# Shift and scale of the first stage as TensorE products with two conditioning columns, in a diffusion block on one core

## The chip, the cores and the metric

The kernel runs on one core of one Trainium2 chip. The metric is the time of one execution on the device in microseconds, as the median of several executions. The execution that the profiler took is a separate one; its own time stands beside them below.

## The reference, cut to what matters

One layer of a diffusion backbone: 1024 latent tokens `x` and 256 context tokens `ctx`, width 1024. Ahead of everything stands an adaptive shift and scale: the conditioning vectors `c` (latent) and `c_ctx` (context) go through SiLU and a matrix `w_ada` of 1024 by 6144, which gives six vectors of 1024; the first two are the shift and the scale of the token mixer's input.

```python
silu_c = jax.nn.silu(c)
silu_cc = jax.nn.silu(c_ctx)
sh_m, sc_m, g_m, sh_f, sc_f, g_f = jnp.split((silu_c @ w_ada[l] + b_ada[l])[:, None, :], 6, axis=-1)
csh_m, csc_m, ... = jnp.split(silu_cc @ w_ada[l] + b_ada[l], 6, axis=-1)
y, y_c = token_mixer(x * (1.0 + sc_m) + sh_m, xc * (1.0 + csc_m) + csh_m, w_in[l], ...)
```

The mixer begins with one large input projection of the modulated tokens, `h @ w_in` (59 blocks of 128 output channels), whose parts feed neighbourhood attention, a recurrent branch and a gated branch; a merge, a norm and a gated feed-forward follow. The latent stream needs all six vectors, the context only the first two, since it is dropped after the mixer.

## The kernel before, in words

Activations lie with 128 channels on the partitions and tokens along the free axis, so the 1024 channels are eight tiles, numbered k = 0 to 7. Every number that enters a large product is split into a high part and a low part (`hh` and `hl` for the latent tile, `ch` and `cl` for the context tile, `wh` and `wl` for a weight block), and each product is three matmuls: high by high, low by high, high by low.

`phase0a` is the first stage. For each tile k it loads two blocks `w` of 128 rows of the transposed `w_ada` (the scale's and the shift's), and the tiles `x` and `xc`. The four numbers per channel (`mod`: scale and shift, each for latent and context) come from VectorE: `ada_row` multiplies a block of 128 by 1024 with a copy of SiLU(c) or SiLU(c_ctx) on all partitions (`cb`) and sums along the row. ScalarE then writes `hh` (rounded) and overwrites `x` with the modulated value, and GpSimd takes the difference, `hl`. The loop also begins the first projections as the tiles come: `FIRST` holds blocks 36 to 39, one of which is loaded and split in each of the passes k = 0 to 3 (`L234`, `L237`), and their products are accumulated in PSUM at lines L306 to L308. Three of these pairs of accumulators come from the six banks called `d`, the fourth from the two called `gr`.

After the loop the other projections run in the order of the list `ms`, each with lines L220 to L222; ScalarE evicts them (L444, L526 and others), VectorE shifts and mixes them along the tokens, and side work for the recurrent branch is put into TensorE's stream behind a later projection. VectorE also works off the other 32 blocks of `w_ada` there, two tiles `wa` in flight, with the same `ada_row`.

A scheduler decides in which order each engine gets its instructions when the program is built. Each engine takes its own in that order and waits where a semaphore says so. Loads are issued by the SyncE queue, in order as well. Tiles come from pools with a fixed number of buffers: 6 for `w5` (the `w` blocks here), 2 for `x`, 2 for `xc`, 2 for `wr` (raw weights), 2 banks for `gr`.

Of the kernel before, what the change touches and what calls it, by code (L numbers as in the profile page):

```python
# [15 lines left out]
P = 128  # L16
D = 1024
S = 1024
CT = 256
NT = S + CT  # L20
KT = D // P
# [7 lines left out]
COLS = (24, 32, 32, 24)  # L29
BOFF = {(0, 0): 0, (0, 1): 264, (0, 3): 616, (1, 0): 880, (1, 1): 1168, (1, 3): 1552}  # L30
NBIAS = 1840
FIRST = (36, 37, 38, 39)
LATE = 3
NWA, NW5, NT2 = 2, 6, 8
LEAD, LAG, AHEAD = 2, 2, 5
NPP, NPT = 4, 3
SIDE = 16
# [19 lines left out]
class Kern:  # L57
# [178 lines left out]
            hi_eng.tensor_copy(hi, src)  # L236
        (lo_eng or nc.vector).tensor_tensor(lo, src, hi.bitcast(F32), ALU.subtract)  # L237

    def ada_row(self, w, q, start, o, out):
        self.nc.vector.tensor_tensor_reduce(out, w, self.cb[q], 1.0, start, ALU.mult, ALU.add, o)  # L240


    def phase0a(self):
        nc, a, c, v = self.nc, self.a, self.c, self.v
        tp, hp = self.tp, self.hp
        self.cb = []
        one = self.bp.tile([1, P], F32, name="one")
        nc.vector.memset(one, 1.0)
        for q in range(2):
            t = (self.bp if q else tp).tile([P, D], F32, name=f"cb{q}")  # L250
            if q == 0:
                nc.sync.dma_start(t, a["crow"][:, 0:D].to_broadcast([P, D]))
                nc.scalar.activation(t, t, AF.Silu)
            for i in range(0, D * q, 512):
                cr = self.t2()
                nc.sync.dma_start(cr[0:1], a["crow"][:, D * q + i:D * q + i + 512])
                ps = self.dps()
                nc.tensor.matmul(ps, one, cr[0:1], start=True, stop=True)
                nc.scalar.activation(t[:, i:i + 512], ps, AF.Silu)
            self.cb.append(t)  # L260
        self.h = []
        self.hc = []
        bada = v("bada")
        first = {}
        for k in range(KT):
            x = self.bp.tile([P, S], F32, name="x", tag="x", bufs=2)
            xc = self.bp.tile([P, CT], F32, name="xc", tag="xc", bufs=2)
            m = self.cp.tile([P, 4], F32, name=f"mod{k}")
            w = [self.w5()[:, 0:D] for _ in range(2)]
            for i in range(2):  # L270
                nc.sync.dma_start(w[i], a["wada"][8 - 8 * i + k])
            for q in range(2):
                for i, b in enumerate((c["bsc"], bada)):
                    junk = w[i] if q else self.bp.tile([P, D], F32, name="junk", tag="junk", bufs=1)
                    self.ada_row(w[i], q, b[:, k:k + 1], m[:, 2 * i + q:2 * i + q + 1], junk)
            nc.sync.dma_start(x, a["xT"][k])
            nc.sync.dma_start(xc, a["cT"][k])
            hh = hp.tile([P, S], F32R, name=f"hh{k}")
            hl = hp.tile([P, S], F32R, name=f"hl{k}")
            ch = tp.tile([P, CT], F32R, name=f"ch{k}")  # L280
            cl = tp.tile([P, CT], F32R, name=f"cl{k}")
            for (xi, hi, lo, q, n) in ((x, hh, hl, 0, S), (xc, ch, cl, 1, CT)):
                sc_, sh_ = m[:, q:q + 1], m[:, 2 + q:3 + q]
                nc.scalar.activation(hi, xi, AF.Identity, scale=sc_, bias=sh_)
                nc.scalar.activation(xi, xi, AF.Identity, scale=sc_, bias=sh_)
                nc.gpsimd.tensor_tensor(lo, xi, hi.bitcast(F32), ALU.subtract)
            self.h.append((hh, hl))
            self.hc.append((ch, cl))
            if k < 4:
                z = FIRST[k]  # L290
                raw = self.raw()
                nc.sync.dma_start(raw, a["win"][z])
                w = [self.bp.tile([P, D], F32R, name=f"w{k}{i}") if k >= 2 else
                     self.wp.tile([P, D], F32R, name=n, tag=n, bufs=2) for i, n in enumerate(("wh", "wl"))]
                self.split(w[0], w[1], raw, nc.gpsimd)
                pss = [self.dps() for _ in range(2)] if k < 3 else [
                    self.ps.tile([P, 512], F32, name="gr", tag="gr", bufs=self.ngr) for _ in range(2)]
                first[z] = w + [pss]
            for i, (z, (wh, wl, pss)) in enumerate(first.items()):
                for k2 in range(0 if i == k else k, k + 1):  # L300
                    q = slice(P * k2, P * k2 + P)
                    hh, hl = self.h[k2]
                    xs = (self.hc[k2], (hh[:, 0:512], hl[:, 0:512]), (hh[:, 512:S], hl[:, 512:S]))
                    for p, (xh, xl) in zip(pss, xs[3 - len(pss):]):
                        p = p[:, 0:xh.shape[1]]
                        nc.tensor.matmul(p, wh[:, q], xh, start=(k2 == 0), stop=False)  # L306
                        nc.tensor.matmul(p, wh[:, q], xl, start=False, stop=False)
                        nc.tensor.matmul(p, wl[:, q], xh, start=False, stop=(k2 == KT - 1))  # L308
        self.first = {z: w[2] for z, w in first.items()}
        self.cm_b.__exit__(None, None, None)  # L310
        self.cm_b, self.bp = self.pool("lora", side="right")
        self.lora_weights()
        ones = tp.tile([P, 64], F32, name="ones")
        nc.gpsimd.memset(ones, 1.0)
        self.ws, self.bs = tp.tile([P, 8, P], F32, name="sws"), tp.tile([P, 4, P], F32, name="sbs")
        nc.sync.dma_start(self.ws, a["sws"])
        ps = self.ps.tile([P, 4, P], F32, name="gr", tag="gr", bufs=self.ngr)
        for e in range(2):
            nc.sync.dma_start(self.bs[64 * e:64 * e + 64], a["sbs"][e].unsqueeze(0).to_broadcast([64, 4, P]))
            nc.tensor.matmul(ps[64 * e:64 * e + 64], ones, self.ws[:, e:8:2, :], start=True, stop=True)  # L320
        for g in range(4):
            nc.vector.scalar_tensor_tensor(self.bs[:, g, :], ps[:, g, :], v("sb")[:, g:g + 1], self.bs[:, g, :], ALU.mult, ALU.add)
        ms = list(FIRST) + [48, 49]
        for j in range(4):
            ms += [40 + j, 28 + j] + [55 + 2 * j] * (j < 2) + [44 + j, 32 + j] + [56 + 2 * j] * (j < 2) + [51, 52] * (j == 3)
        ms += [53, 54, 50]
        na = 16
        self.late = []
        for i, m in enumerate(ms):
            late, self.late = self.late[:LATE], self.late[LATE:]  # L330
            (self.proj_gelu if m > 50 else self.proj_rwkv if m >= 36 else self.proj_kv)(m)
            self.run_late(late)
            for _ in range(2):
                if i >= 6 and na < 48:
                    w = tp.tile([P, D], F32, name="wa", tag="wa", bufs=NWA)
                    nc.sync.dma_start(w, a["wada"][na])
                    self.ada_row(w, 0, bada[:, na:na + 1], self.ada[:, na:na + 1], w)
                    na += 1
        self.run_late(self.late)
        self.ada_rest()  # L340
# [1025 lines left out]
def host(i):  # L1366
    c = np.ascontiguousarray
    f = {k: np.asarray(v) for k, v in i.items()}
    o = {}
# [9 lines left out]
    o["wout"] = c(f["w_out"][0].reshape(KT, P, D))  # L1379
    o["wdn"] = c(f["ffn_w_down"][0].reshape(NFF, P, D))  # L1380
    o["ln1"] = c(np.stack([f["ln1_g"][0], f["ln1_b"][0]]))
    o["wada"] = c(f["w_ada"][0].T.reshape(48, P, D))
    o["crow"] = c(np.concatenate([f["c"][0], f["c_ctx"]])[None])
    o["wbr"] = c(np.concatenate([wt(f["w_branch"][0, b]) for b in range(3)]))
    pv = np.zeros((P, NPV), np.float32)

# [28 lines left out]
    for (rb, cb), off in BOFF.items():  # L1415
        w = COLS[cb]
# [34 lines left out]
```

## Time and profile before

| what | value |
|---|---|
| median of 3 executions | 2448.16 us (2442.55 to 2451.53) |
| the profiled execution | 2457.49 us |
| its span | 2455.7 us |
| mean granted TensorE clock | 0.973 |
| TensorE matmul busy | 2350.8 us, 96% of the span |
| VectorE busy | 1606.1 us, 65% |
| ScalarE busy | 914.9 us, 37% |
| GpSimd busy | 681.1 us, 28% |

The profiled execution lies 9.3 us over the median of the others. PE is TensorE's matmul side and PEld its weight loads, which overlap; DVE is VectorE, ACT ScalarE, POOL GpSimd, SP the queue that issues loads. A row of a group gives line, engine, operation, `out<-in` tiles, shapes and count, then busy time and mean nanoseconds of one, then the idle time of the engine just before. A row of the timeline gives start, duration, engine, line, operation and tiles, with the idle time ahead in brackets. TensorE starts a matmul before the one ahead has ended, so the cost of one in a dense run is the distance between starts, not its duration. PEclk is the clock that the throttle granted, as a share of the full one; ahead of its first recorded change the record shows 1.00 whatever the clock was.

### The profile page before, as it was taken

To read this page: it belongs to the slowest core of one execution; us is meant where nothing else is said; L and a number is where in the kernel's file an instruction comes from. 1 tells how busy PE (TensorE), PEld (TensorE's weight loads), DVE (VectorE), ACT (ScalarE), POOL (GpSimd) and SP (SyncE) were. 2 spreads that over 40 slices of the span, in tenths; PEclk is the share of its full clock that TensorE was granted. 3 is DMA by queue.
4 is the path that set the end of the run, shared out by engine and by line. 5 is a ranking of instruction groups with operands and counts; after the bars stand their busy time and mean duration, and the time that the engine had idled before them with its cause. 6 is when DMAs were issued, how large, how long until landed. Compare 5 with 4: busy or idle time off the path is not lost.

```text
span 2455.7 us, 39343 instructions
## 1 busy us (share of the span) xinstructions
PE 2350.8 (96%) x14520; PEld 1850.5 (75%) x14520; DVE 1606.1 (65%) x3498; ACT 914.9 (37%) x1845; POOL 681.1 (28%) x714
## 2 busy tenths in 40 slices
PE   6999999999999999999999999999889999999997
PEld 4778888776777776677777778778678888887886
DVE  8884446347786778778358873778575555555835
ACT  4443334232343443344345552233433333333321
POOL 6221213441211111211121131142434333425402
PEclk9999999999897999999999999999889999999999
DMA  7675434553342343433277547655223222237551
GB/s 252 208 236 166 140 125 155 167 165 87 98 100 70 100 104 100 104 93 73 66 195 196 173 149 267 192 175 172 78 82 98 78 78 78 86 131 273 166 167 52
DMA packets 276116, 337.44 MB, mean 137 GB/s; under 512 B 123314, under 2 KB 194226, under 8 KB 275924
## 3 DMA queue, kind: packets, MB, share of 16 engines
q1 hardware_dynamic: 208804, 240.91, 33.1%
q10 hardware_dynamic: 54608, 51.40, 6.9%
q0 software_dynamic: 12512, 42.62, 4.7%
q8 instruction: 115, 1.88, 0.3%
q14 instruction: 77, 0.63, 0.1%
HBM read 248.85 MB, written 85.99 MB: 136 GB/s over the span
## 4 chain that ended last, share of the span: by engine, by line
PE 64%; DVE 8%; DMA 4%; issue 3%; ACT 2%; POOL 1%; SPq 0%; DVEq 0%; ACTq 0%; POOLq 0%
PE d L221 10%; PE d L222 10%; PE d L220 10%; PE d L1012 3%; PE pv L896 3%; PE d L1013 3%; PE d L1011 3%; PE ho L731 2%; PE gr L656 2%; PE sc L748 2%; PE pt L882 2%; PE sc L743 1%; PE sc L756 1%; PE gr L655 1%; PE sc L754 1%
## 5 line engine op out<-in xcount | busy, mean ns | idle before, releaser
L221 PE MATMUL d<-hl,wh 128*128 128x512 f32 x1056 | 435.8, 413 | 0.0
L222 PE MATMUL d<-hh,wl 128*128 128x512 f32 x1056 | 434.8, 412 | 0.0
L220 PE MATMUL d<-hh,wh 128*128 128x512 f32 x1056 | 433.8, 411 | 0.0
L221 PEld LDWEIGHTS d<-hl,wh 128*128 128x128 f32 x1056 | 202.1, 191 | 42.4 <-issue 0.7
L222 PEld LDWEIGHTS d<-hh,wl 128*128 128x128 f32 x1056 | 202.1, 191 | 42.3 <-issue 2.0
L220 PEld LDWEIGHTS d<-hh,wh 128*128 128x128 f32 x1056 | 201.9, 191 | 41.2 <-issue 1.6
L212 DVE TENSOR_TENSOR wl<-wr,wh 128x1024 fp32r<-128x1024 f32 x51 | 64.9, 1273 | 159.0 <-ACT wh L208 110.6
L208 ACT ACTIVATE wh<-wr 128x1024 fp32r<-128x1024 f32 x79 | 83.6, 1058 | 194.9 <-PE d L221 160.4
L212 POOL TENSOR_TENSOR wl<-wr,wh 128x256 fp32r<-128x256 f32 x112 | 85.6, 795 | 251.1 <-ACT wh L208 197.1
L237 DVE TENSOR_TENSOR o<-wr,o 128x1024 fp32r<-128x1024 f32 (+1 forms) x64 | 93.5, 1463 | 21.4 <-ACT o L234 21.0
L1012 PE MATMUL d<-dl,ah 128*128 128x512 f32 x252 | 98.7, 392 | 2.2 <-DVE dl L237 2.2
L768 ACT ACTIVATE rv<-sc,E 64x64 f32<-64x64 f32 x152 | 46.5, 308 | 143.2 <-DVE rv L767 131.9
L1011 PE MATMUL d<-dh,ah 128*128 128x512 f32 x252 | 98.8, 392 | 0.0
L1013 PE MATMUL d<-dh,al 128*128 128x512 f32 x252 | 98.7, 392 | 0.0
L234 ACT ACTIVATE o<-wr 128x1024 fp32r<-128x1024 f32 (+1 forms) x64 | 59.2, 926 | 104.0 <-PE d L221 73.1
L896 PE MATMUL pv<-pT,V 128*64 128x128 f32 (+2 forms) x640 | 92.1, 284 | 0.0
L237 DVE TENSOR_TENSOR al<-ar,ah 128x512 fp32r<-128x512 f32 x42 | 40.6, 981 | 78.3 <-ACT ah L234 78.3
L1006 POOL TENSOR_TENSOR wl<-wr,wh 128x1024 fp32r<-128x1024 f32 x16 | 42.6, 2661 | 169.0 <-ACT wh L1005 125.5
L734 DVE TENSOR_TENSOR X<-ho,Dt 48x192 f32<-48x192 f32 (+2 forms) x240 | 68.3, 285 | 24.3 <-PE ho L731 19.6
L1239 POOL TENSOR_TENSOR act<-act 128x512 f32<-128x512 f32 x22 | 28.8, 1309 | 193.9 <-issue 160.2
L896 PEld LDWEIGHTS pv<-pT,V 128*64 128x64 f32 (+2 forms) x640 | 69.1, 138 | 16.4 <-issue 10.8
L767 DVE TENSOR_SCALAR rv<-sc,E 64x64 f32<-64x64 f32 x152 | 41.8, 275 | 56.0 <-PE sc L756 38.9
(402 smaller groups left out, 6123.0 us busy)
## 6 DMA issues: line engine op xcount, KB each, us to landing
wr<-wgu SPq DMA_DIRECT2D x45, 512.0 KB
dr<-wdn SPq DMA_DIRECT2D x42, 512.0 KB
wa<-wada SPq DMA_DIRECT2D x32, 512.0 KB
wr<-win SPq DMA_DIRECT2D x31, 512.0 KB
wr<-win ACTq DMA_DIRECT2D x28, 512.0 KB
s_gt<-stg ACTq DMA_DIRECT2D x48, 256.0 KB
wr<-wbr SPq DMA_DIRECT2D x24, 512.0 KB
g<-s_gt SPq DMA_DIRECT2D x48, 256.0 KB
```

Of the source, the lines that this page charges most:

```text
L208: nc.scalar.activation(hi[:, :n], raw[:, :n], AF.Copy)
L212: (lo_eng or self.lo_eng).tensor_tensor(lo[:, q], raw[:, q], hi[:, q].bitcast(F32), ALU.subtract)
L220: nc.tensor.matmul(ps, w, xh, start=first and k == 0, stop=False)
L221: nc.tensor.matmul(ps, w, xl, start=False, stop=False)
L222: self.last = nc.tensor.matmul(ps, lo[:, P * k:P * k + P], xh, start=False, stop=last and k == n - 1)
L234: nc.scalar.activation(hi, src, AF.Copy)
L237: (lo_eng or nc.vector).tensor_tensor(lo, src, hi.bitcast(F32), ALU.subtract)
L734: nc.vector.tensor_tensor(X[z:z + n, :, t0:64], e[z:z + n], Dt[z:z + n, :, t0:64], ALU.add)
L896: nc.tensor.matmul(o, V[0:k, vt, 64 * e:64 * e + 64], pt[0:k, i, :], start=(i == 0), stop=(i == len(cols) - 1))
L1011: nc.tensor.matmul(ps, xh, wh, start=first, stop=False)
L1012: nc.tensor.matmul(ps, xh, wl, start=False, stop=False)
L1013: nc.tensor.matmul(ps, xl, wh, start=False, stop=last)
```

## The change

The four numbers per channel now come from TensorE. `cc` holds the two conditioning vectors as columns (128 partitions, 8 tiles of channels, 2 columns), after SiLU. Each pass of the loop still loads two blocks of 128 by 1024, from a layout `wadk` in which a block holds, for 128 output channels, the eight 128 by 128 pieces that a matmul takes as weights. Eight matmuls with a moving operand of two columns accumulate one block's result in PSUM, in a `gr` bank, and VectorE adds the bias (L263). The low parts `hl` and `cl` go from GpSimd to VectorE. `FIRST` has three blocks, and block 39 becomes an ordinary projection behind them. `x` and `xc` get four buffers each. The broadcast copy `cb` is made only of `c`, after the loop, for the 32 later blocks.

```diff
-FIRST = (36, 37, 38, 39)
+FIRST = (36, 37, 38)
-NWA, NW5, NT2 = 2, 6, 8
+NWA, NW5, NT2, NX = 2, 6, 8, 4
...
+        cc = self.bp.tile([P, KT, 2], F32, name="cc")
+        nc.sync.dma_start(cc, a["ccol"])
+        nc.scalar.activation(cc, cc, AF.Silu)
...
         for k in range(KT):
-            x = self.bp.tile([P, S], F32, name="x", tag="x", bufs=2)
-            xc = self.bp.tile([P, CT], F32, name="xc", tag="xc", bufs=2)
+            x = self.bp.tile([P, S], F32, name="x", tag="x", bufs=NX)
+            xc = self.bp.tile([P, CT], F32, name="xc", tag="xc", bufs=NX)
             m = self.cp.tile([P, 4], F32, name=f"mod{k}")
-            w = [self.w5()[:, 0:D] for _ in range(2)]
-            for i in range(2):
-                nc.sync.dma_start(w[i], a["wada"][8 - 8 * i + k])
-            for q in range(2):
-                for i, b in enumerate((c["bsc"], bada)):
-                    junk = w[i] if q else self.bp.tile([P, D], F32, name="junk", tag="junk", bufs=1)
-                    self.ada_row(w[i], q, b[:, k:k + 1], m[:, 2 * i + q:2 * i + q + 1], junk)
+            pm = self.ps.tile([P, 512], F32, name="gr", tag="gr", bufs=self.ngr)
+            for i, b in enumerate((c["bsc"], v("bada"))):
+                w = self.w5()[:, 0:D]
+                nc.sync.dma_start(w, a["wadk"][8 - 8 * i + k])
+                for k2 in range(KT):
+                    nc.tensor.matmul(pm[:, 2 * i:2 * i + 2], w[:, P * k2:P * k2 + P], cc[:, k2, :],
+                                     start=(k2 == 0), stop=(k2 == KT - 1))
+                nc.vector.tensor_scalar(m[:, 2 * i:2 * i + 2], pm[:, 2 * i:2 * i + 2], b[:, k:k + 1], None, ALU.add)
...
-                nc.gpsimd.tensor_tensor(lo, xi, hi.bitcast(F32), ALU.subtract)
+                nc.vector.tensor_tensor(lo, xi, hi.bitcast(F32), ALU.subtract)
...
-            if k < 4:
+            if k < len(FIRST):
...
-        ms = list(FIRST) + [48, 49]
+        ms = list(FIRST) + [39, 48, 49]
...
+        self.cb = tp.tile([P, D], F32, name="cb")
+        nc.sync.dma_start(self.cb, a["crow"].to_broadcast([P, D]))
+        nc.scalar.activation(self.cb, self.cb, AF.Silu)
```

Lines after `phase0a` move up by ten: L444 of before is L434 of the changed kernel, L402 is L392, while L208 to L237 stay.

TensorE's stream, at the start of the program. Before:

```order
L258 MATMUL d<-t_226,one 128x512
L258 MATMUL d<-t_231,one 128x512
L306 MATMUL d<-hh_251,wh 128x512
L307 MATMUL d<-hl_252,wh 128x512
L308 MATMUL d<-hh_251,wl 128x512
L306 MATMUL d<-hh_251,wh 128x512
```

And now (`w_227` and `w_238` are tile 0's two blocks, `w_279` and `w_290` tile 1's, `w_343` is tile 2's first; `hh_251` is tile 0, `hh_303` tile 1):

```order
L261 MATMUL gr<-cc,w_227 128x2 x8
L261 MATMUL gr<-cc,w_238 128x2 x8
L261 MATMUL gr<-cc,w_279 128x2 x8
L293 MATMUL d<-hh_251,wh 128x512
L294 MATMUL d<-hl_252,wh 128x512
L293 MATMUL d<-hh_251,wh 128x512
L295 MATMUL d<-hh_251,wl 128x512
L294 MATMUL d<-hl_252,wh 128x512
L295 MATMUL d<-hh_251,wl 128x512
L261 MATMUL gr<-cc,w_290 128x2 x8
L293 MATMUL d<-hh_303,wh 128x512 x2
L261 MATMUL gr<-cc,w_343 128x2 x8
```

Three groups of eight narrow matmuls stand ahead of the first wide one, and tile 1's second group stands behind tile 0's wide ones, which need `wl`.

TensorE's stream between tiles 3 and 4. Before, tile 4 (`hh_479`) follows directly on tile 3, with 24 wide matmuls, the first of them:

```order
L306 MATMUL d<-hh_479,wh 128x512
L307 MATMUL d<-hl_480,wh 128x512
L308 MATMUL d<-hh_479,wl 128x512
L306 MATMUL d<-hh_479,wh 128x512
L307 MATMUL d<-hl_480,wh 128x512
```

Now (`w_475` and `w_486` belong to tile 4, `w_531` and `w_542` to tile 5, `w_587` and `w_598` to tile 6; `hh_443` is tile 3 and `hh_499` tile 4):

```order
L295 MATMUL d<-hh_443,w_380 128x512
L261 MATMUL gr<-cc,w_475 128x2 x8
L261 MATMUL gr<-cc,w_531 128x2 x8
L261 MATMUL gr<-cc,w_486 128x2 x8
L261 MATMUL gr<-cc,w_542 128x2 x8
L293 MATMUL d<-hh_499,wh 128x512 x4
L293 MATMUL d<-hh_499,w_379 128x512 x2
L261 MATMUL gr<-cc,w_587 128x2 x8
L261 MATMUL gr<-cc,w_598 128x2 x8
L294 MATMUL d<-hl_500,wh 128x512
```

Six groups of narrow matmuls stand nearly in a row there, with six wide ones between them. Behind them come 48 wide ones, tile 7's two groups, and tile 7's 18 wide ones.

ScalarE's stream where the loop ends and the next projection's weights are split (`wh`, L208). Before:

```order
L285 ACTIVATE xc<-xc,mod_613 128x256
L444 ACTIVATE w_703<-d 128x512 x2
L444 ACTIVATE w_711<-d 128x512 x2
L208 ACTIVATE wh<-wr 128x1024
L402 ACTIVATE lwh_668<-w_675 128x1024
```

And now:

```order
L273 ACTIVATE xc<-xc,mod_641 128x256
L434 ACTIVATE w_741<-d 128x512 x2
L434 ACTIVATE w_749<-d 128x512
L317 ACTIVATE cb<-cb 128x1024
L392 ACTIVATE lwh_703<-w_710 128x1024
L392 ACTIVATE lwh_704<-w_717 128x1024
L434 ACTIVATE w_749<-d 128x512
L208 ACTIVATE wh<-wr 128x1024 x2
```

The split of the next weights stands behind `cb` and the two `lwh` now, where it stood ahead of them.

More of the change, by code (lines that the diff above doesn't have):

```diff
@@ L237, in split, with ada_row @@
         (lo_eng or nc.vector).tensor_tensor(lo, src, hi.bitcast(F32), ALU.subtract)
-    def ada_row(self, w, q, start, o, out):
-        self.nc.vector.tensor_tensor_reduce(out, w, self.cb[q], 1.0, start, ALU.mult, ALU.add, o)
+    def ada_row(self, w, start, o):
+        self.nc.vector.tensor_tensor_reduce(w, w, self.cb, 1.0, start, ALU.mult, ALU.add, o)
     def phase0a(self):
@@ L245, in phase0a @@
         tp, hp = self.tp, self.hp
-        self.cb = []
-        one = self.bp.tile([1, P], F32, name="one")
-        nc.vector.memset(one, 1.0)
-        for q in range(2):
[L250 to L260, printed above, removed]
+        cc = self.bp.tile([P, KT, 2], F32, name="cc")
@@ L261, in phase0a @@
+        nc.sync.dma_start(cc, a["ccol"])
+        nc.scalar.activation(cc, cc, AF.Silu)
         self.h = []
         self.hc = []
-        bada = v("bada")
         first = {}
         for k in range(KT):
-            x = self.bp.tile([P, S], F32, name="x", tag="x", bufs=2)
-            xc = self.bp.tile([P, CT], F32, name="xc", tag="xc", bufs=2)
+            x = self.bp.tile([P, S], F32, name="x", tag="x", bufs=NX)
+            xc = self.bp.tile([P, CT], F32, name="xc", tag="xc", bufs=NX)
             m = self.cp.tile([P, 4], F32, name=f"mod{k}")
-            w = [self.w5()[:, 0:D] for _ in range(2)]
-            for i in range(2):
-                nc.sync.dma_start(w[i], a["wada"][8 - 8 * i + k])
-            for q in range(2):
-                for i, b in enumerate((c["bsc"], bada)):
-                    junk = w[i] if q else self.bp.tile([P, D], F32, name="junk", tag="junk", bufs=1)
-                    self.ada_row(w[i], q, b[:, k:k + 1], m[:, 2 * i + q:2 * i + q + 1], junk)
+            pm = self.ps.tile([P, 512], F32, name="gr", tag="gr", bufs=self.ngr)
[6 more added lines that the diff above has]
+                nc.vector.tensor_scalar(m[:, 2 * i:2 * i + 2], pm[:, 2 * i:2 * i + 2], b[:, k:k + 1], None, ALU.add)
@@ L295, in phase0a @@
                 self.split(w[0], w[1], raw, nc.gpsimd)
-                pss = [self.dps() for _ in range(2)] if k < 3 else [
-                    self.ps.tile([P, 512], F32, name="gr", tag="gr", bufs=self.ngr) for _ in range(2)]
+                pss = [self.dps() for _ in range(2)]
                 first[z] = w + [pss]
@@ L335, in phase0a @@
                     w = tp.tile([P, D], F32, name="wa", tag="wa", bufs=NWA)
-                    nc.sync.dma_start(w, a["wada"][na])
-                    self.ada_row(w, 0, bada[:, na:na + 1], self.ada[:, na:na + 1], w)
+                    nc.sync.dma_start(w, a["wada"][na - 16])
+                    self.ada_row(w, v("bada")[:, na:na + 1], self.ada[:, na:na + 1])
                     na += 1
@@ L1381, in host @@
     o["ln1"] = c(np.stack([f["ln1_g"][0], f["ln1_b"][0]]))
-    o["wada"] = c(f["w_ada"][0].T.reshape(48, P, D))
-    o["crow"] = c(np.concatenate([f["c"][0], f["c_ctx"]])[None])
+    o["wadk"] = wt(f["w_ada"][0][:, 0:2 * D])
+    o["wada"] = c(f["w_ada"][0][:, 2 * D:].T.reshape(32, P, D))
+    o["crow"] = c(f["c"])
+    o["ccol"] = c(np.stack([f["c"][0], f["c_ctx"]]).reshape(2, KT, P).transpose(2, 1, 0))
     o["wbr"] = c(np.concatenate([wt(f["w_branch"][0, b]) for b in range(3)]))
```

## The prediction

> **What bounds the kernel now.** I read the stages first, each with its span and the busy time of PE, PEld, DVE, ACT and POOL, then the granted clock, the DMA share and its rate.
>
> ```profile
> 0.00:20.00 20.00, 6.15 (x8) 2.45 (x9) 12.20 (x21) 7.95 (x9) 8.16 (x10) 1.00 0.92 324
> 20.00:40.00 20.00, 12.75 (x36) 8.16 (x36) 19.86 (x19) 8.94 (x10) 16.29 (x7) 1.00 0.66 231
> 40.00:60.00 20.00, 18.29 (x79) 14.40 (x78) 19.82 (x21) 9.71 (x11) 12.85 (x6) 1.00 0.60 195
> 60.00:84.00 24.00, 19.43 (x80) 15.35 (x79) 17.94 (x20) 13.66 (x18) 12.25 (x7) 0.93 0.69 227
> 100.00:140.00 40.00, 40.00 (x209) 34.03 (x208) 37.01 (x48) 13.73 (x17) 1.46 (x2) 1.00 0.71 198
> 200.00:500.00 300.00, 297.11 (x1560) 246.50 (x1559) 132.78 (x177) 103.36 (x160) 81.24 (x113) 1.00 0.45 143
> ```
>
> From 100 us on TensorE hardly stops, so what the first stage gains or loses stays to the end. In the first 84 us it is busy for 56.6 us and VectorE is full from 20 us on. The waits and groups of these 84 us say why.
>
> ```profile
> ACT hh L284 <- DVE mod L240: 32.4, 8, 6.6
> PE d L307 <- POOL hl L286: 11.0, 7, 3.6
> L240 DVE CUSTOM_DVE_ANT_0 w<-w,cb,der 128x1024 f32<-128x1024 f32 x8 | 20.2, 2528 | 0.2
> L240 DVE CUSTOM_DVE_ANT_0 junk<-w,cb,c_pv 128x1024 f32<-128x1024 f32 x8 | 20.1, 2506 | 0.0
> L240 DVE CUSTOM_DVE_ANT_0 w<-w,cb,c_pv 128x1024 f32<-128x1024 f32 x8 | 13.3, 1666 | 0.2
> L240 DVE CUSTOM_DVE_ANT_0 junk<-w,cb,der 128x1024 f32<-128x1024 f32 x8 | 12.7, 1592 | 5.2 <-DMA w<-wada 5.2
> ```
>
> ScalarE waits 32.4 us for the scales, and these are 66.3 us of VectorE. The stage is bound by `ada_row`. TensorE's rows show two rates and where the stage ends:
>
> ```profile
> 14.92 0.80 PE L306 MATMUL d<-hh,wh 128*128 128x512 f32 x1 [4.80 <-ACT wh L234]
> 19.78 0.63 PE L306 MATMUL d<-hh,wh 128*128 128x512 f32 x1
> 20.21 0.63 PE L307 MATMUL d<-hl,wh 128*128 128x512 f32 x1
> 83.47 0.39 PE L308 MATMUL gr<-hh,w 128*128 128x512 f32 x1
> 83.70 0.28 PE L220 MATMUL d<-ch,wh 128*128 128x256 f32 x1
> ```
>
> Starts are 0.43 us apart at 20 us and 0.23 (0.228 over a long run) at 83, so the clock is at half early on (the record's 1.00 there is its default). The stage ends at 83.7 with 192 wide matmuls done.
>
> **The change part by part.** *Removed:* the 66.3 us of `ada_row`, and with them the waits above; the two matmuls that build the context's `cb`. *Added to TensorE:* 16 groups of 8 products, 128 by 128 weights with two columns. The trace has this very shape, in the readout:
>
> ```profile
> 1280.38 1.84 PE L951 MATMUL pt<-c_pv,A 128*128 128x2 f32 x16
> 1282.09 0.48 PE L222 MATMUL d<-hh,wl 128*128 128x512 f32 x1
> L320 PE MATMUL gr<-sws,ones 128*64 128x512 f32 x4 | 1.1, 618 | 0.0
> ```
>
> Eight products are 16 matmuls there and take 1282.09 - 1280.38 = 1.71 us, as much as 7.5 wide ones. Sixteen groups: 27.4 us at full clock. Against this the loop loses one of four early projections, 48 x 0.228 = 10.9 us, which only moves behind it. So TensorE has 144 x 0.228 + 27.4 = 60.2 us in the stage where it had 43.8. To break even the stage must end at 83.7 - 10.9 + 1.0 = 73.8 us (the 1.0 are the matmuls for the gating weights, L320, which came behind the loop and now stand inside it).
>
> At half clock the group is dearer, if the weight loads halve too. The nearest rows have 64 columns, once at full and once at half clock:
>
> ```profile
> 626.61 0.39 PE L755 MATMUL sc<-rv,KKo 128*128 128x64 f32 x2
> 626.84 0.44 PE L756 MATMUL sc<-ub,BB 128*128 128x128 f32 x2
> 780.28 0.63 PE L755 MATMUL sc<-rv,KKo 128*128 128x64 f32 x2
> 780.71 0.74 PE L756 MATMUL sc<-ub,BB 128*128 128x128 f32 x2
> ```
>
> The two of L755 take 0.23 us, then 0.43: about double, so a group is between 1.71 (nothing doubles) and 3.42 us at half clock; I take 3.42, since these are loads of the same size. The Trainium skill (TensorE: Matmul & The Clock Gate, LDWEIGHTS) gives a weight load as columns / 1.2 ns, 107 ns for 128, with no word of the clock. By that a group costs 1.71 us at either clock and the sum below would end about 16 us earlier; the 0.43 speaks against it.
>
> *Which clock the groups run at* is the main unknown. In the recurrent stage narrow matmuls keep TensorE full for long, and the clock is still not granted:
>
> ```profile
> 768.00:772.00 4.00, 4.00 (x32) 3.41 (x29) 2.10 (x8) 1.31 (x5) 0.00 (x0) 0.50 0.21 55
> ...
> 784.00:788.00 4.00, 4.00 (x23) 2.65 (x22) 1.29 (x8) 0.22 (x1) 0.00 (x0) 0.50 0.00 0
> 64.27 0.80 PE L307 MATMUL d<-hl,wh 128*128 128x512 f32 x1 [3.07 <-POOL hl L286]
> 66.99 0.48 PE L307 MATMUL d<-hl,wh 128*128 128x512 f32 x1
> ```
>
> The last two rows show that one 3 us gap costs the clock (0.80 us for a matmul), and that wide matmuls have won it back some 2.7 us later. I infer that a group of two columns counts like a gap: after about 4 us of groups the clock halves, and 3.4 to 6.8 us of wide matmuls (5 taken) bring it back.
>
> *The walk.* Durations besides:
>
> ```profile
> L284 ACT ACTIVATE hh<-x,mod 128x1024 fp32r<-128x1024 f32 x8 | 9.9, 1242 | 32.4 <-DVE mod L240 32.4
> L284 ACT ACTIVATE ch<-xc,mod 128x256 fp32r<-128x256 f32 x8 | 4.7, 588 | 0.7 <-DVE mod L240 0.7
> 15.82 3.31 POOL L237 TENSOR_TENSOR wl<-wr,wh 128x1024 fp32r<-128x1024 f32 x1
> 13.51 2.35 POOL L286 TENSOR_TENSOR hl<-x,hh 128x1024 fp32r<-128x1024 f32 x1 [10.78 <-ACT x L285]
> 6.37 3.75 PE L258 MATMUL d<-t,one 1*128 1x512 f32 x4 [6.37 <-DMA t<-crow]
> 8.00:12.00 4.00, 2.12 (x3) 0.33 (x1) 3.71 (x7) 2.28 (x3) 0.00 (x0) 1.00 1.04 413
> 85.46 1.22 DVE L212 TENSOR_TENSOR wl<-wr,wh 128x1024 fp32r<-128x1024 f32 x1
> L234 ACT ACTIVATE wh<-wr 128x1024 fp32r<-128x1024 f32 x2 | 2.1, 1040 | 0.0
> 82.61 1.99 ACT L402 ACTIVATE lwh<-w 128x1024 fp32r<-128x1024 f32 x2
> 86.73 0.38 PE L222 MATMUL d<-ch,wl 128*128 128x256 f32 x1 [1.71 <-DVE wl L212]
> ```
>
> Loads run at 413 GB/s when asked, 0.52 MB in 1.3 us, so with four `x` in flight the first weights are there at about 6.5 us (the first small loads land at 6.37 now) and a tile's 1.7 MB each 4 us; they wait on nothing later. After a group VectorE must read the bank before the other half may be written. No row shows this hand-over; I take 0.5 us, and since it lies on the path some six times, half or double of it moves the sum by 2 to 3 us.
>
> - To 38 us, half clock throughout. Groups from 6.5 to 9.9, 10.4 to 13.9 and on to 17.3. ScalarE gets the scales at 14.4 and does `hh` 1.24, `ch` 0.59, the same for `x` and `xc`, `wh` 1.04: 19.1. GpSimd makes `wl` (2.35 to 3.31, 2.8 taken): 21.9. Six wide to 23.2, group to 26.6, wait for `hh` to 28.5, group and 18 wide to 38.0, where 16 in a row have won the clock.
> - Tiles 2 and 3: group to 39.7, wait for `hh` to 41.6, four wide, two groups of which one and a half at half clock, to 49.6. Then 44 wide, 8 of them slow at first, to 61.3.
> - Tiles 4 to 6: four groups, about the last at half clock, 69.6; six slow wide 72.2; two slow groups 79.6; 48 wide, 11 slow, 92.5.
> - Tile 7: two groups 96.5, scale and `hh` 98.4, 18 mostly slow wide: about 106.
>
> Summed otherwise: start 6.5, wide 32.8, groups 27.4, waits 11, about nine slow groups 16, some 64 slow wide matmuls at 0.2 more 13: 106.7. The loop ends near 106 instead of 73.8: +32.
>
> *After the loop.* ScalarE splits the next weights behind `cb` (1.04 us, as `wh` of that size) and two `lwh` (1.99), which stood behind them. Before, TensorE lost 1.71 us there; now I count 3.2 us until `wh` plus some 2.5 for a clock lost again (5 us of wide matmuls at half rate): +4. The moved projection's low part on VectorE (1.22 us instead of GpSimd's 3.3) is hidden: TensorE has 10.9 us of work beside it. `hl` on VectorE, 8 x 1.22, is in the walk, in the 66.3 us that came free. The later `wada` loads keep their count and their two buffers; they meet TensorE once, at 143 us, where the order of five more of them ahead may cost or save as much as is lost there now:
>
> ```profile
> DVE wa L240 <- DMA wa<-wada: 11.1, 5, 5.5
> PE gr L466 <- DVE w L460: 4.3, 1, 4.3
> ```
>
> I put it at nothing, with 8 us to either side (the 4.3 and the half clock behind it). Sum: +32 + 4 = +36 us on the profiled 2457.5, that is 2493.5; the median of the runs is 9.3 lower, so 2484.
>
> **The rivals.** *The clock stays granted over the groups.* The Trainium skill (TensorE: Matmul & The Clock Gate, The HAM clock gate) has the gate follow how busy the engine has been over a window of some 3.4 us. By that rule the 10 us of groups at the start would win the clock. As a mechanism of this kernel, with weight loads counting as work: half clock only to about 11 us and briefly after the longer waits; the walk of above, redone with 1.71 a group from there, ends at 88. +14, and +2 after the loop: 2464. For it: nothing here is as dense as these groups. Against: the rows at 768 to 788. Even at full clock from the first moment the walk ends at 84.6, since tile 0's chain of scale, `hh`, `x`, `wh` and `wl` holds the in-order stream until 18.5 and each tile waits once more: +13 with the 2.
>
> *The loop becomes bound by its work alone, and the kernel faster.* Start 6.5 and 60.2 of work, if loads in flight hide the waits and the clock holds: 66.7, seven under 73.8, so 2441. It decides where waits and slow clock together stay under 7.1 us. Against it: groups, VectorE's read and ScalarE's pass stand one behind the other ahead of each of the first three tiles, and the waits alone are 11 us in the walk.
>
> *The change lands within 0.5%,* 12 us, which is about what a measurement of this kernel can tell from no change: the full-clock walk, and the loss at 143 us saved. 2456.
>
> **How the numbers follow.** Forecast 0.65 (its own range 2470 to 2500: the clock's return at 3.4 or 6.8 us, 8 us at 143). Clock granted 0.2, at 2464. Within 0.5% 0.09, faster 0.06. The range from 2458 takes in the granted clock; its upper end 2500 takes slower returns. Slower 0.85.
>
> **What would show it.** Right: L261 at about 107 ns a matmul at full clock and 213 at half; granted clock at half over the groups before tiles 4 and 7; VectorE nearly idle in the first 80 us; the first L220 at about 106 to 110 us; all behind it shifted alike. Wrong: wide matmuls at 0.23 us right behind the groups (then the rival), or the first L220 before 74 us.

## The result, and the profile after

The changed kernel takes 2488.48 us (median of 4 executions, 2479.19 to 2498.33) against 2449.73 us (4 executions, 2442.55 to 2451.53). The ratio is 1.0147 with a 95% interval of 1.0111 to 1.0183: slower by 1.5%, which is 36 us; the two medians lie 38.8 us apart. The profiled execution of the changed kernel took 2479.19 us, 21.7 more than the profiled one before; where the 14 us between 36 and 22 went is told below, in the section on why the prediction was right.

The stages of the changed kernel, with the columns of the first table of the prediction (PE, PEld, DVE, ACT, POOL with their counts, granted clock, DMA share, GB/s):

```profile
0.00:20.00 20.00, 12.18 (x51) 11.22 (x51) 2.84 (x14) 5.80 (x7) 3.79 (x8) 1.00 0.85 318
20.00:40.00 20.00, 16.55 (x70) 14.83 (x71) 2.22 (x5) 5.89 (x7) 2.59 (x2) 1.00 0.65 231
60.00:84.00 24.00, 23.68 (x117) 21.78 (x117) 5.81 (x12) 9.96 (x12) 0.00 (x0) 0.64 0.81 257
100.00:140.00 40.00, 35.45 (x157) 28.08 (x154) 27.99 (x35) 12.48 (x18) 2.83 (x6) 0.88 0.52 171
```

VectorE, full from 20 us on in the kernel before, now works 2.2 of 20 us. TensorE is busy for 23.68 of 24 us at 60, and its clock there is 0.64: the bound has moved, and to an engine that runs at two thirds of its speed.

The waits of the first 105 us, as engine, tile and line waited for, then total us, times and longest:

```profile
DVE mod L263 <- PE gr L261: 66.6, 15, 10.0
ACT hh L272 <- DVE mod L263: 65.9, 7, 13.8
PE d L293 <- ACT hh L272: 4.8, 3, 1.6
```

VectorE waits 66 us for TensorE's groups, and ScalarE as long for the scales that VectorE reads out of them; before, ScalarE waited 32.4 us for VectorE's rows. TensorE itself waits little. In the timeline of its rows (start, duration, tiles, count, idle time ahead in brackets) the groups and the end of the loop read:

```profile
5.77 3.55 PE L261 MATMUL gr<-cc,w 128*128 128x2 f32 x16 [5.77 <-DMA w<-wadk]
27.74 3.41 PE L261 MATMUL gr<-cc,w 128*128 128x2 f32 x16
39.70 1.21 PE L293 MATMUL d<-hh,wh 128*128 128x512 f32 x4 [1.58 <-ACT hh L272]
59.45 8.62 PE L261 MATMUL gr<-cc,w 128*128 128x2 f32 x64
74.36 3.57 PE L261 MATMUL gr<-cc,w 128*128 128x2 f32 x16 [0.32 <-DVE mod L263]
90.83 1.84 PE L261 MATMUL gr<-cc,w 128*128 128x2 f32 x16
104.49 0.39 PE L295 MATMUL d<-hh,w 128*128 128x512 f32 x1
108.47 0.50 PE L220 MATMUL d<-hh,wh 128*128 128x512 f32 x1 [3.59 <-ACT wh L208]
111.21 0.79 PE L222 MATMUL d<-hh,wl 128*128 128x512 f32 x1 [0.96 <-DVE wl L212]
184.07 2.60 PE L456 MATMUL gr<-w,c_blk 128*128 128x256 f32 x4 [4.15 <-DVE w L450]
```

A group of 16 matmuls takes 3.41 us at 27.74 and 1.84 at 90.83. The loop's last wide matmul starts at 104.49 (83.47 before), and two stops of TensorE follow before the next projection runs freely. The last row, L456, is the first matmul of a norm in the projections behind the loop, where TensorE stops again; in the kernel before it is L466, at 147.51. I call this place the norm.

To compare kernels I use one place behind all of this, the first matmul of the gating unit (`gr<-sws,w`). In every kernel here it comes after the same projections, and the profiles have the same 12576 matmuls from it on. I call it the mark. A line's own row gives it, as the first of the two start times; the kernel before stands first, the changed one second:

```profile
L502 PE MATMUL gr<-sws,w x128: 272/273/323, 440.3 to 486.9; 128*64 128x128 f32 x128
L492 PE MATMUL gr<-sws,w x128: 272/273/323, 476.0 to 520.7; 128*64 128x128 f32 x128
```

The mark comes 35.7 us later. The mark is the better measure of this change: the four executions of the changed kernel lie 19 us apart, and the work behind the mark alone varies by 29 us between the profiles (below). For runs with a single execution I therefore argue from the mark and the loop's end, not from the total. How far the mark itself moves from one execution to the next is not measured, since each kernel has one profile; two kernels with the same loop ended it 2.1 us apart, so a difference of a few us at the mark says little.

### The profile page after: what moved, and what is told of

It reads as the page before. It is cut to its first block, busy times and chain, and to the rows that moved or that the text cites. A ratio compares the mean times of both kernels' runs of the same rounds, so it can differ in the third digit from the quotient of the medians.

```text
span 2477.4 us, 39794 instructions
## 1 busy us (share of the span) xinstructions
PE 2383.6 (96%) x14772; PEld 1888.1 (76%) x14772; DVE 1556.0 (63%) x3466; ACT 911.7 (37%) x1844; POOL 638.4 (26%) x697
## 3 DMA queue, kind: packets, MB, share of 16 engines
q1 hardware_dynamic: 208944, 240.91, 32.4%
## 4 chain that ended last, share of the span: by engine, by line
PE 64%; DVE 8%; DMA 3%; issue 2%; POOL 2%; ACT 2%; ACTq 0%; SPq 0%; DVEq 0%; POOLq 0%
PE d L221 11%; PE d L222 11%; PE d L220 10%; PE d L1002 3%; PE d L1003 3%; PE pv L886 3%; PE d L1001 3%; PE ho L721 2%; PE sc L738 2%; PE gr L646 2%; PE pt L872 1%; PE sc L733 1%; PE sc L746 1%; PE gr L645 1%; PE sc L744 1%
## 5 line engine op out<-in xcount | busy, mean ns | idle before, releaser
L220 PE MATMUL d<-hh,wh 128*128 128x512 f32 x1072 | 439.4, 410 | 3.6 <-ACT wh L208 3.6
L222 PE MATMUL d<-hh,wl 128*128 128x512 f32 x1072 | 440.9, 411 | 1.0 <-DVE wl L212 1.0
L221 PE MATMUL d<-hl,wh 128*128 128x512 f32 x1072 | 441.5, 412 | 0.0
L208 ACT ACTIVATE wh<-wr 128x1024 fp32r<-128x1024 f32 x80 | 84.5, 1058 | 194.6 <-PE d L221 147.9
L237 DVE TENSOR_TENSOR o<-wr,o 128x1024 fp32r<-128x1024 f32 (+1 forms) x64 | 93.8, 1467 | 22.3 <-ACT o L234 21.9
L237 DVE TENSOR_TENSOR al<-ar,ah 128x512 fp32r<-128x512 f32 x42 | 40.6, 982 | 78.5 <-ACT ah L234 78.3
L222 PE MATMUL d<-o,wl 128*128 128x512 f32 x192 | 75.3, 395 | 1.3 <-DVE wl L212 1.2
```

The source lines that it names most:

```text
L208: nc.scalar.activation(hi[:, :n], raw[:, :n], AF.Copy)
L220: nc.tensor.matmul(ps, w, xh, start=first and k == 0, stop=False)
L221: nc.tensor.matmul(ps, w, xl, start=False, stop=False)
L222: self.last = nc.tensor.matmul(ps, lo[:, P * k:P * k + P], xh, start=False, stop=last and k == n - 1)
```

## The experiments

**The moved projection alone.** My theory: the removed 66 us of rows were the bound, and what TensorE does in the loop is what replaces them. To split the 35.7 us I first did the smallest part of the change alone, in the kernel before.

```diff
-FIRST = (36, 37, 38, 39)
+FIRST = (36, 37, 38)
...
-            if k < 4:
+            if k < len(FIRST):
...
-        ms = list(FIRST) + [48, 49]
+        ms = list(FIRST) + [39, 48, 49]
```

> The kernel before with one edit of the change alone: three early projections, the fourth moved behind the loop. My theory (the stage before is bound by VectorE's scales, so the moved projection takes no time out of it, and its 48 x 0.228 = 10.9 us come back behind the loop): the loop's last wide matmul at 82 to 84 us as before, and the first matmul of the gating unit in the recurrent stage's start (440.3 us before) at 449 to 451. Rival (the four projections also set the end of the loop, so taking one out shortens it): the loop ends at 73 to 78 and the mark stays at 440 to 443.

TensorE's rows around the end of the loop and at the norm, then the mark:

```profile
78.98 0.40 PE L308 MATMUL d<-hh,w 128*128 128x512 f32 x1
...
84.20 0.50 PE L220 MATMUL d<-hh,wh 128*128 128x512 f32 x1 [3.82 <-ACT wh L208]
90.89 0.50 PE L222 MATMUL d<-hh,wl 128*128 128x512 f32 x1 [2.92 <-DVE wl L212]
164.71 2.93 PE L466 MATMUL gr<-w,c_blk 128*128 128x256 f32 x4 [6.76 <-DVE w L460]
```

```profile
L502 PE MATMUL gr<-sws,w x128: 272/273/324, 458.4 to 505.0; 128*64 128x128 f32 x128
```

Neither number came. The loop ends 4.5 us earlier, between the two expectations, and the mark is 18.1 us later, beyond both. So this edit alone, in a loop that VectorE binds, costs half of the change's 35.7 us, and more than the 10.9 us of its work: 10.9 - 4.5 leaves 6.4, the stop for `wh` 3.8 is new, that for `wl` 1.2 longer than the 1.71 before, that at the norm 2.4 longer than 4.34. These make 13.8. Most of the remaining 4.3 is the clock: between the loop's end and the mark it stands at half for 13.7 us (84.8 to 88.2, 91.6 to 95.0, 163.3 to 170.1) against 6.8 in the kernel before, which costs 3.4, and a stop at 216.9 takes 0.6. The total, 2475.03 us in one execution, agrees with the mark.

**The low parts on VectorE.** The change takes `hl` and `cl` off GpSimd. Done alone, it tells whether the rows of `ada_row` were slow because of GpSimd. The second kernel moves the low parts of the early weight blocks too (the last two lines of the diff), so that GpSimd has nothing left in the loop.

```diff
-                nc.gpsimd.tensor_tensor(lo, xi, hi.bitcast(F32), ALU.subtract)
+                nc.vector.tensor_tensor(lo, xi, hi.bitcast(F32), ALU.subtract)
...
-                self.split(w[0], w[1], raw, nc.gpsimd)
+                self.split(w[0], w[1], raw, nc.vector)
```

> The kernel before with another edit of the change alone: the low parts hl and cl on VectorE instead of GpSimd, VectorE still making the scales. Theory (VectorE's 66 us of scales are slow because GpSimd works beside them: 1.28 us for one in stretches without GpSimd, up to 3.3 beside it): 32 x 1.28 = 41, 8 x (1.22 + 0.42) = 13 and some 6 beside GpSimd's wl, so the loop ends at 74 to 78 us instead of 83.7 and the kernel is 6 to 10 us faster. Rival (a scale costs what it costs, and the engine that is full gets 13 us more): the loop ends at 92 to 97 and the kernel is 8 to 13 us slower.

> As the run with hl and cl on VectorE, and the low parts wl of the four early weight tiles there too, so that GpSimd does nothing in the loop. Theory: 41 + 13 + 4 x 1.22 = 59 us of VectorE from about 9 us on and one or two waits for ScalarE; the loop ends at 70 to 75, and the kernel is 9 to 13 us faster than before. Rival (as there): the loop ends near 97 to 100 and the kernel is 13 to 16 us slower.

Of the first kernel the groups of `ada_row` in the first 84 us (total, mean ns), and of the second one of them, the loop's last matmul and the mark:

```profile
L240 DVE CUSTOM_DVE_ANT_0 junk<-w,cb,der 128x1024 f32<-128x1024 f32 x8 | 14.5, 1816 | 5.3 <-DMA w<-wada 5.3
L240 DVE CUSTOM_DVE_ANT_0 w<-w,cb,c_pv 128x1024 f32<-128x1024 f32 x8 | 10.2, 1281 | 0.1
L240 DVE CUSTOM_DVE_ANT_0 w<-w,cb,der 128x1024 f32<-128x1024 f32 x8 | 10.2, 1278 | 0.0
L240 DVE CUSTOM_DVE_ANT_0 junk<-w,cb,c_pv 128x1024 f32<-128x1024 f32 x8 | 10.2, 1278 | 0.0
```

```profile
L240 DVE CUSTOM_DVE_ANT_0 junk<-w,cb,der 128x1024 f32<-128x1024 f32 x8 | 10.2, 1281 | 5.7 <-DMA w<-wada 5.7
...
68.66 0.39 PE L308 MATMUL gr<-hh,w 128*128 128x512 f32 x1
...
L502 PE MATMUL gr<-sws,w x128: 272/273/324, 430.6 to 475.6; 128*64 128x128 f32 x128
```

The rows fall from 66.3 us to 45.1 and then to 41: with GpSimd out, each takes 1.28 us. The theory holds, the rival falls. The loops end at 75.1 and 68.7, the second earlier than expected. Part is given back behind the loop. The first kernel's mark is at 440.3, as before (its norm now waits 6.84 us), and its ratio is 0.9991 (0.9961 to 1.0021): no difference, where 6 to 10 us were expected. The second kernel's mark is 9.7 us earlier, at the low end of what was expected, and its ratio 0.9954 (0.9927 to 0.9981), 2440.1 against 2449.8 us. It beats both kernels: what helps is to take GpSimd out of VectorE's way altogether, one step further than the change goes (it leaves `wl` on GpSimd), and it needs no TensorE product.

**The low parts back on GpSimd, in the changed kernel.** The reverse edit.

> The changed kernel with the low parts hl and cl back on GpSimd. Theory (2.35 instead of 1.22 us for hl, with VectorE idle anyway; the first tiles wait for it, the later ones have other matmuls to run): the loop ends 3 to 6 us later than 104.7, and the mark in the recurrent stage (476.0) goes to 479 to 482. Rival (moving them is what the change gains: each of eight tiles pays the difference): 9 to 12 us later.

The loop ends at 106.28 instead of 104.49, less than expected, and the mark is at 488.2, 12.2 us later: beyond what I expected and just over the rival's 9 to 12, but not for its reason. The eight tiles cost 1.8 us together; the rest comes behind the loop, where the stops are 7.9 us longer and the clock stands at half for 6.9 us more, 3.4 us of loss:

```profile
117.79 0.80 PE L222 MATMUL d<-hh,wl 128*128 128x512 f32 x1 [2.79 <-DVE wl L212]
194.31 2.93 PE L456 MATMUL gr<-w,c_blk 128*128 128x256 f32 x4 [9.32 <-DVE w L450]
189.50:199.60 10.10, 5.29 (x15) 3.88 (x15) 8.48 (x12) 2.34 (x3) 0.00 (x0) 0.50 0.61 185
```

The last row is the stage around the norm, 10 us at half clock. Its stop of 9.32 us was 4.15 in the changed kernel. VectorE's rows ahead of it wait for loads of `w_ada` for 15.1 us in 60, against 10.6 there; why they wait longer here I have not isolated, and with one execution chance is not out.

**No products.** To price the groups with all that hangs on them, I left them out: VectorE adds the bias to the first two columns of the loaded block.

```diff
-                for k2 in range(KT):
-                    nc.tensor.matmul(pm[:, 2 * i:2 * i + 2], w[:, P * k2:P * k2 + P], cc[:, k2, :],
-                                     start=(k2 == 0), stop=(k2 == KT - 1))
-                nc.vector.tensor_scalar(m[:, 2 * i:2 * i + 2], pm[:, 2 * i:2 * i + 2], b[:, k:k + 1], None, ALU.add)
+                nc.vector.tensor_scalar(m[:, 2 * i:2 * i + 2], w[:, 0:2], b[:, k:k + 1], None, ALU.add)
```

> The changed kernel without the 16 groups of products: VectorE adds the bias to the first two columns of the loaded weight tile instead, so all loads stay and shift and scale are other numbers. Theory (groups, the clock that they cost and the waits behind them carry the whole stage): 32.8 us of wide matmuls are left, and the loop is then bound by the loads, 1.7 MB a tile and 4 to 4.6 us each, or by ScalarE's 3.7 to 4.7 us a tile; the loop ends at 46 to 56 us. Rival (the stage is bound by ScalarE and the hand-overs, and the groups run beside them): the loop ends above 75.

```profile
55.14 0.40 PE L291 MATMUL d<-hh,w 128*128 128x512 f32 x1
L488 PE MATMUL gr<-sws,w x128: 272/273/323, 435.0 to 479.8; 128*64 128x128 f32 x128
```

The loop's last matmul starts at 55.14 us, 49.4 earlier, and the mark is at 435.0, 41.0 earlier. So the 16 groups carry the stage: 27.4 us of them at full clock, and 22 more of clock and waits. Behind the loop 8 us are given back: the stop for `wh` is 4.76 instead of 3.59 and that at the norm 8.73 instead of 4.15, and half clock lasts 17.1 us between the loop's end and the mark instead of 10.2.

**Wide matmuls between the groups.** Is it the clock? I added work whose result nothing uses: 10 wide matmuls ahead of the first group and 5 ahead of each other one.

```diff
+                for _ in range(10 if k + i == 0 else 5):
+                    nc.tensor.matmul(pm[:, 8:512], dz[:, 0:P], dz[:, 8:512], start=True, stop=True)
                 for k2 in range(KT):
```

> The changed kernel with unused work added on TensorE: before the first group of products 10, before each of the other fifteen groups 5 wide matmuls (504 columns) from a constant tile, 85 in all, about 0.225 us each at full clock: 19 us more work in the loop. Theory (the streamed columns hold the clock; a group of two columns counts as idle, and the clock at half costs about 9 slow groups x 1.71 = 16 us and some 60 slow wide matmuls x 0.2 = 12 us in the changed kernel): the clock is full from about 12 us on, the groups take 1.71 us, and the loop ends at 92 to 106 us, no later than the 104.7 of the changed kernel in spite of the added work. Rival (the groups' 3.4 us are not a matter of what TensorE streams, or the clock falls anyway): the loop ends at 120 to 130.

Two groups, the stage from 33.6 us on, the loop's end, and the mark:

```profile
6.30 1.84 PE L267 MATMUL gr<-cc,w 128*128 128x2 f32 x16
55.70 1.84 PE L267 MATMUL gr<-cc,w 128*128 128x2 f32 x16
33.60:91.50 57.90, 57.01 (x339) 49.28 (x337) 10.78 (x24) 18.11 (x22) 0.00 (x0) 1.00 0.47 157
97.26 0.39 PE L301 MATMUL d<-hh,w 128*128 128x512 f32 x1
L498 PE MATMUL gr<-sws,w x128: 272/273/323, 466.9 to 511.4; 128*64 128x128 f32 x128
```

With 85 matmuls more, some 19 us of work, the loop ends 7.2 us earlier and the mark comes 9.1 us earlier. The clock stays full for 58 us in a row in which the groups' rows read 1.84, as they do at full clock. So it is the clock, and what holds it is how much TensorE streams. It was not full from 12 us on, as I had expected: it fell twice in the first two tiles (16.5 to 19.9 and 23.3 to 33.5 us), and what tipped it there I have not isolated. The kernel is still slower than the one before at the mark (466.9 against 440.3): the added work eats most of what the clock returns.

**One-pass products.** The operands are rounded to the one-pass type, so a product is one matmul instead of two. VectorE copies each weight block ahead of its group, and two `x` are in flight.

```diff
+                r = self.bp.tile([P, D], F32R, name="wf", tag="wf", bufs=2)
+                nc.vector.tensor_copy(r, w)
                 for k2 in range(KT):
-                    nc.tensor.matmul(pm[:, 2 * i:2 * i + 2], w[:, P * k2:P * k2 + P], cc[:, k2, :],
+                    nc.tensor.matmul(pm[:, 2 * i:2 * i + 2], r[:, P * k2:P * k2 + P], cc[:, k2, :],
```

> The changed kernel with the products of shift and scale from operands rounded to the one-pass type (a copy of each weight tile by VectorE, about 1.2 us and ahead of its group, and two x in flight to make room): one matmul for a product instead of two. Theory (a group costs the weight loads of its matmuls, 107 ns each at full and 213 at half clock): a group takes 0.86 us at full and 1.71 at half clock; 13.7 us of products gone, some 8 us of half clock with them, 1 to 2 us lost at the start for the first copies; the loop ends at 80 to 88 us instead of 104.7. Rival (a group costs its columns, its accumulation or the reads behind it, not the number of loads): a group stays above 1.4 us at full clock and the loop ends at 96 to 105.

```profile
43.78 0.95 PE L264 MATMUL gr<-cc,wf 128*128 128x2 f32 x8
26.98 1.70 PE L264 MATMUL gr<-cc,wf 128*128 128x2 f32 x8
85.54 0.39 PE L298 MATMUL d<-hh,w 128*128 128x512 f32 x1
L495 PE MATMUL gr<-sws,w x128: 272/273/323, 455.0 to 499.6; 128*64 128x128 f32 x128
```

A group of 8 matmuls takes half as long, at full clock (0.95) and at half (1.70); the loop ends at 85.5 and the mark is 21.0 us earlier. The price of a group goes with the number of its matmuls, each with its load of 128 columns; the rival falls. The run doesn't separate the load from some fixed cost of a matmul. These groups too lose the clock (0.79 from 60 to 84 us), so the two-pass type isn't what loses it.

**Two input tiles in flight,** `NX = 2` in the changed kernel.

> The changed kernel with two input tiles x in flight, as in the kernel before. Theory (a tile's turn takes 9 to 14 us on TensorE and its loads 4 to 4.6, so loads are early either way): the loop ends at 103 to 107 and the mark in the recurrent stage (476.0 us) moves by less than 2 us. Rival (four in flight are what keeps TensorE fed): 5 us or more later.

The loop's last matmul starts at 108.52 and the mark is at 481.4, 4.0 and 5.4 us later: the first number misses what I expected by 1.5, the second by 3.4, and the second is on the rival's side. No row shows TensorE waiting for a load behind the first block. What differs is the clock:

```profile
40.00:60.00 20.00, 18.81 (x72) 16.40 (x73) 3.47 (x6) 7.24 (x9) 2.35 (x1) 0.66 0.42 153
60.00:84.00 24.00, 23.69 (x114) 22.57 (x113) 3.17 (x9) 6.71 (x8) 0.00 (x0) 0.59 0.27 84
```

0.66 and 0.59 against 0.74 and 0.64. The next run has the changed kernel's loop untouched, and there it ends at 106.58, 2.1 us later than in the profile above. So two of the four us are within what the loop does by itself from one execution to the next. Whether the others belong to the buffers stays open: the theory isn't confirmed, and the rival's reason, a TensorE short of loads, has no row for it.

**The 32 later rows held back.** A stop at the norm came in every kernel so far, of 3.5 us (one-pass products) to 9.3 us. In the changed kernel the rows that remain on VectorE start three projections later here, and a copy of one column keeps each load from starting early.

```diff
-                if i >= 6 and na < 48:
+                if i >= 9 and na < 48:
                     w = tp.tile([P, D], F32, name="wa", tag="wa", bufs=NWA)
+                    nc.gpsimd.tensor_copy(w[:, 0:1], self.hi[:, 0:1].bitcast(F32))
                     nc.sync.dma_start(w, a["wada"][na - 16])
```

> The changed kernel with the other 32 rows of shift and scale held back: they start three projections later, and one GpSimd copy of a weight column into each buffer ahead of its load keeps the load (and so the row) behind that projection's weights. Theory (TensorE's wait for the square ahead of the norm, 4.15 us at 184 in the changed kernel, 4.34 in the one before, comes from the rows that stand ahead of it on VectorE; these rows are work of the same kind as the 16 that the change took away): the wait falls under 1 us, the half clock behind it (3.4 us) goes, and the mark in the recurrent stage goes from 476.0 to 467 to 471. Rival (the projection's own chain on VectorE makes the square late): a wait of 3 us or more stays and the mark moves by less than 2 us.

The stop at the norm is gone, as the theory has it; counted against this run's own loop, 2.1 us later, the matmuls from 250 to 400 us come about 5 us earlier. But the mark is at 481.4. A stop of 7 us has come up just ahead of it, where ScalarE waits for a buffer that a store to memory frees (TensorE's waits to 500 us, the longest):

```profile
PE gr L370 <- ACT t L372: 8.9, 2, 7.1
434.07 1.09 ACT L372 ACTIVATE t<-gr 128x512 f32<-128x512 f32 x2 [8.13 <-DMA s_li<-t]
432.40:439.00 6.60, 4.28 (x17) 4.04 (x18) 4.55 (x5) 2.94 (x7) 3.32 (x4) 0.50 1.04 381
```

The rows cause the stop at the norm, but held back they bring another; the DMA share of 1.04 at that place suggests that their loads collide with the stores, which I did not isolate.

**All of it together, in the kernel before:** the low parts on VectorE, the rows held back, and the low-rank and gating weights split behind the sixth projection.

```diff
-        self.lora_weights()
+        self.lora_tiles()
...
+            if i == 5:
+                self.lora_weights()
...
-                if i >= 6 and na < 48:
+                if i >= 9 and na < 48:
+                    nc.gpsimd.tensor_copy(w[:, 0:1], self.hi[:, 0:1].bitcast(F32))
```

> The kernel before with the low parts on VectorE (hl, cl and wl, as in the faster run), and behind the loop two orders changed: the weights of the low-rank steps and of the gating unit are loaded and split behind the sixth projection instead of ahead of the fifth, and the other 32 rows of shift and scale are held back as in the run above. Theory (a TensorE stop behind the loop costs its length and the half clock after it, about twice): in the run with the low parts alone 3.6 us of waits and 6.8 us at half clock stood at 69 to 81, 4.6 us and 6.8 at 133 to 143; without them the mark in the recurrent stage (440.3 before, 430.6 there) comes at 416 to 424, and the kernel is 0.7 to 1.1 per cent faster than before. Rival (the next late piece takes each wait's place): the mark stays at 428 or later and the kernel is 0.3 to 0.6 per cent faster.

```profile
388.01 0.69 PE L382 MATMUL gr<-c_ident,w 128*128 128x128 f32 x2 [6.93 <-ACT t L384]
L509 PE MATMUL gr<-sws,w x128: 272/273/323, 434.3 to 479.5; 128*64 128x128 f32 x128
```

The mark is at 434.3, the rival's side, and the ratio 0.9960 (0.9932 to 0.9987), 2441.4 against 2455.2 us: no better than the low parts alone. At 78 us 6.60 us are lost to `wl`, which stands later in VectorE's order. Even so the kernel is 14 us ahead of the one before at 250 us; then 6.93 us and the clock behind them are lost at the same ScalarE line as in the run above, which waits for a buffer that a store frees (`s_kd` here, `s_li` there).

## Why the prediction was right

The forecast was 2484 us, 36 us over the kernel before, by TensorE's groups at half clock. Measured: 2488, and 35.7 us at the mark. The mechanism is the one forecast: without the groups the loop ends 49.4 us earlier, and with wide matmuls between them the clock is full from 33.6 us to the loop's last tile. That the sum came out to the microsecond is in part luck, as the steps show:

- *Start and groups.* The first weights were there at 5.77 us (6.5 taken), a group takes 1.71 us at full clock and 3.41 at half (1.71 and 3.42). The range of a half-clock group had its lower end at 1.71; the higher end, taken from the two rows with 64 columns, is right. The rule of the Trainium skill (TensorE: Matmul & The Clock Gate, LDWEIGHTS) that a load costs its columns over 1.2, 107 ns here, fits these matmuls at full clock only: 3.41 us for 16 are 213 ns each.
- *Which clock.* The inference that a group counts like a gap was the main one. The stages with borders at the clock's changes show it:

```profile
34.30:41.10 6.80, 5.21 (x34) 4.56 (x33) 0.22 (x1) 2.69 (x3) 0.00 (x0) 1.00 0.27 86
41.20:51.30 10.10, 9.79 (x38) 8.93 (x38) 3.28 (x5) 4.79 (x7) 2.35 (x1) 0.50 0.55 188
51.40:65.00 13.60, 13.60 (x87) 12.14 (x86) 1.61 (x5) 0.00 (x0) 0.00 (x0) 1.00 0.23 69
65.10:82.00 16.90, 16.59 (x62) 15.05 (x63) 4.50 (x9) 9.96 (x12) 0.00 (x0) 0.50 0.97 313
109.40:116.10 6.70, 5.74 (x16) 4.36 (x15) 6.70 (x7) 0.94 (x2) 0.55 (x1) 0.50 0.34 135
```

  From 65 to 82 us TensorE is busy for 16.59 of 16.90 us and gets half the clock. The rival in which the clock follows busy time is out by these rows; the run with added wide matmuls shows the other side. The rule of the Trainium skill on the clock gate (TensorE: Matmul & The Clock Gate, The HAM clock gate), that the gate follows how busy the engine has been, does not agree with these rows.
- *The walk.* The loop's end was to be near 106 and is 104.5 (its last matmul's start): the hand-over cost 0.31 us instead of 0.5 and `wl` 2.35 instead of 2.8, as VectorE was idle. The walk had four groups in a row, the last at half clock, which is 3 x 1.71 + 3.42 = 8.55; the row at 59.45 has 64 matmuls in 8.62. It had the next two at half (74.36: 3.57) and the last two at full (90.83: 1.84). One of the signs that I named was wrong by my own walk: half clock over the groups before tile 7; it came just behind them.
- *After the loop.* +4 was forecast. The stops are 3.59 + 0.96 against 1.71 before, 2.8 us more, and 6.8 us at half clock (109.4 to 116.2) cost 3.4: 6.2. The stop at the norm, put at nothing, is 4.15 against 4.34, and half clock follows it for 3.4 instead of 6.8 us, 1.9 less. Together 21.0 for the loop, 10.9 for the moved projection less 1.0 for L320, 6.2 and -1.9: 35.2 of the measured 35.7. Against the forecast the loop is 1.3 us better, the stops 2.2 worse and the norm 1.9 better; that these nearly cancel is luck.
- *What the sum did not say.* It charged the moved projection with its work. The run with that edit alone shows that it costs 18.1 us where VectorE stays the bound. In the changed kernel the loop's loss and the stops were counted as the walk's and as +4, so the sum came out. Read as shares, the moved projection taken first costs 18 of the 35.7 us, and the products put in the rows' place the other 18. No run has the products with four early projections, so its share in a loop that TensorE fills stays open.
- *The profiled execution* is only 21.7 us longer than the one before. The difference to 35.7 comes up behind the mark, and nothing ties it to the change: in the twelve profiles, one of each kernel, the same 12576 matmuls behind the mark take 1987 to 2016 us, with half clock for 88 to 135 us of them, and the changed kernel and the fastest variant of the one before both have 1987 to 1988. Nine of the 14 us come up in one stretch, here first in the kernel before, then at the same work in the changed one:

```profile
760.00:800.00 40.00, 39.62 (x274) 30.03 (x270) 23.58 (x83) 12.20 (x41) 4.16 (x9) 0.66 0.27 67
795.00:835.00 40.00, 39.51 (x390) 29.51 (x389) 31.80 (x111) 15.66 (x54) 8.02 (x15) 0.91 0.40 107
```

  In 40 us the first has 274 matmuls done at 0.66 of the clock, the second 390 at 0.91. In the recurrent stage the clock is near its edge, and the profiles lose it at other places: behind 500 us the profiled execution before stood at half clock for 124 us, the changed one's for 90. The four executions of the changed kernel fit this: from the shortest to the longest the mean granted clock goes from 0.973 to 0.965, which is some 40 us more at half clock and by my estimate 20 us of time, where 19 were measured. The one-pass kernel, 21.0 us ahead of the changed one at the mark, took 2486.94 us in its one execution. That is why a difference of 20 us needs several executions or a mark.

## What to carry to other kernels

Before you move a reduction from a full engine to one with idle slots, ask whether the receiving work keeps that engine's clock: here a group of 16 narrow matmuls cost as much as 7.5 wide ones at full clock, and twice that where the clock fell. Look first for what makes the full engine slow: here another engine beside it cost 25 of 66 us, and moving that engine's subtractions away gained 0.5% where the products lost 1.5%. A stage that ends earlier is worth less than it says (of 14.8 us in the best version 9.7 arrived), since the work behind it has stops of its own that move.

## What the runs showed of the hardware

- A TensorE that is busy nearly without a gap can lose its clock: in a stretch that begins with groups of two streamed columns it was 0.50 over 17 us with 98% busy time. With 5 wide matmuls ahead of each group it was 1.00 for 58 us on end.
- VectorE's row sums take 1.28 us alone and up to 3.4 beside GpSimd: 66.3 us for 32 before, 45.1 with only the weight blocks' low parts left to GpSimd, 41.0 with nothing left to it. The Trainium skill (SBUF — State Buffer, Who interferes with whom) says that a VectorE instruction with two inputs in SBUF contends with a GpSimd instruction that reads there; these sums have two, and the numbers agree. GpSimd pays as well: its `wl` took 3.31 us beside the sums and 2.35 with VectorE idle.
